# Transposing the latent mixer's probabilities in float32r, from a copy made by DMA

## The chip, the cores and the metric

One core of a Trainium2 chip runs one program. The metric is the device time in microseconds of one execution. The engines of the core are TensorE (PE in the profile, its weight loads PEld), VectorE (DVE), ScalarE (ACT), GpSimd (POOL) and SyncE (SP); DMAs are issued from the queues of SP, ScalarE and GpSimd. TensorE writes to PSUM, and its operands come from the SBUF.

## The reference, cut to what matters

The program runs two blocks on 512 tokens of width 1024 with 256 context tokens. The first block has two layers (attention, a gated linear recurrence, an MLP). The second has two mixers, of which the first is the latent mixer. Queries, keys and values of 16 heads come out of low-rank projections, tokens attend to context and tokens, the context attends to itself, and the result is gated and projected:

```python
def mla_mixer(hc, hx, row, col, w_in, q_norm_g, w_uq, kv_norm_g, w_ukv, w_out):
    ...
    oc = attention_blocks(qc, kc, vc)
    ox = attention_blocks(qx, jnp.concatenate([kc, kx], axis=1), jnp.concatenate([vc, vx], axis=1))

    def out(o, gate):
        b, n = gate.shape[:2]
        return (o.reshape(b, n, MLA_WIDTH) * jax.nn.silu(gate)) @ w_out
```

`attention_blocks` is a softmax of the scores (96 features a head, 32 of them rotated) times the values (64 a head). All arithmetic of the reference is float32. In the kernel the probabilities have to be transposed, because the product with the values contracts over the keys, which then must lie on the partitions.

## The kernel before

Most products are made from operands that are split into two float32r parts, high and low. `split` (L248) copies the high part on ScalarE (L251, L254) and subtracts it on VectorE (L252, L255); `mm3` (L278) makes three TensorE products of each pair, lines L280 to L282. The profile prints float32r operands of TensorE as f32.

`mla` (L1050 and on) has a first stage (low-rank projections and gates) and then the attention, which the change touches. It runs over eight pairs of heads `hp` and, for each, five steps: one for the context (`c` = 1: two tiles of 128 queries against 256 keys, for each head), then four for the tokens (one tile of 128 queries against 768 keys). So there are 40 steps of two heads, and 80 tiles of probabilities `p`. In a step

- `softmax` (L1199) makes the scores of one head into a PSUM tile `S` (L280 to L282), the row maximum on VectorE (`mx`, L1211), the exponential on ScalarE into `p` with its row sum (L1216), the reciprocal of the sum (L1218) and the scaling of `p` in place (L1221), both on VectorE;
- `weigh` (L1225) works on the step before: for each head it transposes `p` in blocks of 128x128 on TensorE into a PSUM tile `T` (L1236; `p` is the weight, the identity streams), copies the result on ScalarE into `pt` (L1237), and then makes the products with the values into `O` (L1244). At the end of a pair's queries the gate `sg` is multiplied in (L1251);
- `prepare` (L1136), in pieces between these, makes keys and queries of the next pair: it loads and splits weights (`raw`, L264, from SP's queue), makes the products into `T` tiles, and moves the rotated part `rot` into `qT` by four small copies within the SBUF, also from SP's queue (L1178).

Buffers: `p` has three, `pt` three, `S` two, `T` three and `O` one. The order of the code gives each instruction its priority. The framework's planner, which knows its own estimates of durations and landings, orders the instructions of each engine and of each DMA queue from that: an instruction whose operands it does not expect to be ready lets others go ahead. On the chip each engine then runs its instructions in this order and waits on semaphores. A TensorE instruction that waits holds those behind it.

The first block has an attention of its own with other functions (L488 and on), whose transposes (L516) the change leaves as they are. There the scores of a float32r product are padded to 256 columns (L489).

Of the kernel before, what the change touches and what calls it, by code (L numbers as in the profile page):

```python
# [11 lines left out]
F32R = mybir.dt.float32r  # L12
I32 = mybir.dt.int32
U32 = mybir.dt.uint32
AF = mybir.ActivationFunctionType
# [177 lines left out]
def f32(ap):  # L193
    return ap.bitcast(F32)
# [855 lines left out]
def mla(P, xs, mod, H, before, keep):  # L1050

    nc, A = P.nc, P.A
# [13 lines left out]
    with ExitStack() as s1:  # L1066
# [33 lines left out]
        for j in range(8):  # L1100
            w = W().rearrange("p s (k n) -> p s k n", k=8)
            for c, o, n in PARTS:
                ps = P.bankA()[:, 0:n]
# [7 lines left out]
    with st as s2:  # L1111
        P.psum(s2, S=(2, 2), T=(3, 1), O=(1, 1))
        kp, pp, one, qp = (P.pool(*x, s2) for x in (("m2k", 3), ("m2p", 3), ("m2o", 1), ("m2q", 4)))
        kTs = [one.tile([96, 2, 768], F32R, name=f"kT{i}") for i in (2, 3, 0, 1)]
        kTs = kTs[2:] + kTs[:2]
        tab = one.tile([128, 512], F32, name="tab")
        nc.sync.dma_start(tab, A["k_gridT"])
        V = [vp.tile([128, 1024], F32, name="V") for _ in range(6)]

# [79 lines left out]
        def softmax(hp, c, t0):  # L1199
            two, m, c0 = (2, 256, 512) if c else (1, 768, 0)  # L1200
            ps = []
            for i in range(2):
                qT, kT = qTs[hp][i], kTs[(2 * hp + i) % 4]
                pss = P.bankS()
                for t in range(two):
                    q = slice(c0 + (t0 + t) * 128, c0 + (t0 + t + 1) * 128)
                    for o, w in ((512, 256),) if c else ((0, 512), (512, 256)):
                        d = pss[:, t * m + o - c0:t * m + o - c0 + w]
                        P.mm3(d, qT[:, 0, q], qT[:, 1, q], kT[:, 0, o:o + w], kT[:, 1, o:o + w], True, True)
                mx = P.sm.tile([128, 2], F32, name="mx")  # L1210
                nc.vector.tensor_reduce(mx[:, 0:two], pss[:, 0:two * m].rearrange("p (t n) -> p t n", t=two),  # L1211
                                        AX.X, OP.max, negate=True)
                p = pp.tile([128, 768], F32, name="p")
                sl = P.sm.tile([128, 2], F32, name="sl")
                for t in range(two):
                    nc.scalar.activation(p[:, t * m:(t + 1) * m], pss[:, t * m:(t + 1) * m], AF.Exp,  # L1216
                                         bias=mx[:, t:t + 1], accum_out=sl[:, t:t + 1])
                nc.vector.reciprocal(sl[:, 0:two], sl[:, 0:two])  # L1218
                for t in range(two):
                    v = p[:, t * m:(t + 1) * m]  # L1220
                    nc.vector.tensor_scalar(v, v, sl[:, t:t + 1], None, op0=OP.mult)  # L1221
                ps.append(p)
                yield ps

        def weigh(hp, c, t0, ps):  # L1225
            two, m, c0 = (2, 256, 512) if c else (1, 768, 0)
            if t0 == 0:
                weigh.o = P.bankO()
            pts = []
            for p in ps:  # L1230
                pt = kp.tile([128, 768], F32, name="pt")
                for o in range(0, two * m, 512):
                    w = min(512, two * m - o)
                    pst = P.bankT()
                    for k in range(0, w, 128):
                        nc.tensor.transpose(pst[:, k:k + 128], p[:, o + k:o + k + 128], P.ident)  # L1236
                    nc.scalar.activation(pt[:, o:o + w], pst[:, 0:w], AF.Copy)  # L1237
                pts.append(pt)
                yield
            for t in range(two):  # L1240
                for k in range(m // 128):
                    for i in range(2):
                        h = 2 * hp + i
                        nc.tensor.matmul(weigh.o[64 * i:64 * i + 64, (t0 + t) * 128:(t0 + t + 1) * 128],  # L1244
                                         V[4 * c + k][:, h * 64:(h + 1) * 64],
                                         pts[i][:, t * m + k * 128:t * m + (k + 1) * 128],
                                         start=(k == 0), stop=(k == m // 128 - 1))
            n = 256 if c else 512
            if (t0 + two) * 128 == n:
                v = sg[hp][:, c0:c0 + n]  # L1250
                nc.vector.tensor_tensor(v, v, weigh.o[:, 0:n], op=OP.mult)  # L1251
# [3 lines left out]
        for hp, c, t in steps:  # L1255
            if c:
                ready = prepare(hp + 1) if hp < 7 else iter(())
            sm = softmax(hp, c, t)
            w = weigh(*before) if before else iter(())
            next(w, None)  # L1260
            for _ in range(2):
                ps = next(sm)
                next(ready, None)
                next(w, None)
            before = (hp, c, t, ps)
        alternate(weigh(*before))


# [325 lines left out]
def program(tc, A, out):  # L1594
    with ExitStack() as ctx:
        P = Prog(tc, A, ctx)
        xs = [P.res.tile([128, 1024], F32, name=f"x{t}") for t in range(4)]
        before, keep = ExitStack(), ExitStack()
        H, mod = first_block(P, xs, P.pool("hx", 1, before))
        finish = mla(P, xs, mod.m[0], H, before, keep)  # L1600
        gla(P, xs, finish, keep, mod.m[1], out)
# [18 lines left out]
```

## Time and profile before

| | |
|---|---|
| median of 3 runs | 2333.55 us (2333.11 to 2333.55) |
| the profiled execution | 2335.07 us, its span 2333.3 us |
| TensorE busy | 2284.1 us, 98% |
| VectorE, ScalarE busy | 1478.0 us (63%), 1063.0 us (46%) |
| DMA | 234.38 MB, mean 100 GB/s |
| attention of the latent mixer | about 1685 to 1935 us of the span |

A busy time adds up the instructions of an engine, overlaps counted once. TensorE's instructions overlap: a product starts while the one before it still runs, so their distance from start to start tells what one costs. A group line gives the count, the busy time, the mean duration of one, and the idle time of the engine just before with what ended it. In a timeline, instructions of one kind that follow each other are merged, with their count and the length from the first start to the last end.

### The profile page before, as it was taken

The page shows a single profiled execution, that of the slowest core. Times are in us where ns is not written, and L with a number is a line of the kernel's source. Part 1 is how long each engine was busy: PE and PEld are TensorE (multiplying, and loading weights), DVE is VectorE, ACT ScalarE, POOL GpSimd, SP SyncE. Part 2 cuts the span into 40 slices and gives each one's busy share as a digit, 9 for nine tenths or more (in the row PEclk, how much of TensorE's full clock was granted, in tenths as well). Part 3 has the DMA queues.
Part 4 walks back from the last instruction along what each step waited for, and adds up shares of the span by engine and source line. Part 5 has one row for each costly group of instructions (what it writes and reads, how often), then busy time and mean ns, then how long its engine had stood idle before and what let it go on. Part 6 is the DMA issues. An engine that isn't in the chain of part 4 may idle for free.

```text
span 2333.3 us, 30784 instructions
## 1 busy us (share of the span) xinstructions
PE 2284.1 (98%) x12108; PEld 1875.9 (80%) x12108; DVE 1478.0 (63%) x2556; ACT 1063.0 (46%) x1958; POOL 71.4 (3%) x120
## 2 busy tenths in 40 slices
PE   8999999999999999999999999999999999999998
PEld 6777878888888777788888888888888888788886
DVE  4477796555555547779645556564478776756586
ACT  3366423444443235642344445452477772563332
POOL 0000000000000000000000000010000000000000
PEclk9999999999999999999999999999999999999999
DMA  4221464555642322146454554212110121121112
GB/s 162 81 73 55 145 212 142 167 130 151 174 100 91 92 81 75 52 155 216 135 172 120 160 164 116 92 54 72 49 31 21 24 74 37 54 81 37 55 46 72
DMA packets 61312, 234.38 MB, mean 100 GB/s; under 512 B 8544, under 2 KB 9840, under 8 KB 54768
## 3 DMA queue, kind: packets, MB, share of 16 engines
q1 hardware_dynamic: 50512, 179.99, 23.3%
q0 software_dynamic: 3456, 25.17, 6.0%
q10 hardware_dynamic: 7200, 27.27, 3.7%
q8 instruction: 95, 1.56, 0.3%
q14 instruction: 49, 0.40, 0.1%
HBM read 227.15 MB, written 2.10 MB: 98 GB/s over the span
## 4 chain that ended last, share of the span: by engine, by line
PE 81%; DVE 10%; ACT 3%; DMA 3%; issue 2%; POOL 1%; SPq 0%; POOLq 0%; ACTq 0%; DVEq 0%
PE A L282 18%; PE A L281 18%; PE A L280 18%; PE S L280 4%; PE S L282 4%; PE S L281 4%; PE O L1244 2%; DVE spl L252 2%; PE T L1236 2%; PE O L522 1%; DMA ada<-in_ada 1%; PE S L496 1%; DVE junk L933 1%; PE T L516 1%; ACT spl L251 1%
## 5 line engine op out<-in xcount | busy, mean ns | idle before, releaser
L280 PE MATMUL A<-big,spl 128*128 128x512 f32 (+1 forms) x1280 | 482.2, 377 | 1.9 <-DVE x L768 1.2
L282 PE MATMUL A<-big,spl 128*128 128x512 f32 (+1 forms) x1280 | 481.0, 376 | 0.2 <-DVE spl L252 0.2
L281 PE MATMUL A<-big,spl 128*128 128x512 f32 (+1 forms) x1280 | 480.1, 375 | 0.0
L252 DVE TENSOR_TENSOR spl<-raw,spl 128x1024 fp32r<-128x1024 f32 (+2 forms) x265 | 317.2, 1200 | 184.0 <-ACT spl L251 182.2
L251 ACT ACTIVATE spl<-raw 128x1024 fp32r<-128x1024 f32 (+2 forms) x265 | 275.2, 1040 | 292.2 <-PE A L282 190.6
L282 PEld LDWEIGHTS A<-big,spl 128*128 128x128 f32 x1280 | 241.2, 188 | 44.6 <-issue 2.6
L280 PEld LDWEIGHTS A<-big,spl 128*128 128x128 f32 x1280 | 241.3, 189 | 43.9 <-DVE x L768 1.6
L281 PEld LDWEIGHTS A<-big,spl 128*128 128x128 f32 x1280 | 241.3, 189 | 42.5 <-issue 1.4
L252 DVE TENSOR_TENSOR spl<-quarter,spl 128x1024 fp32r<-128x1024 f32 x84 | 102.2, 1223 | 144.9 <-ACT spl L251 144.9
L280 PE MATMUL A<-spl,big 128*128 128x512 f32 (+2 forms) x480 | 182.7, 384 | 3.7 <-DVE tg L668 2.1
L281 PE MATMUL A<-spl,big 128*128 128x512 f32 (+2 forms) x480 | 182.3, 381 | 1.4 <-DVE spl L252 0.8
L282 PE MATMUL A<-spl,big 128*128 128x512 f32 (+2 forms) x480 | 181.7, 380 | 0.2 <-DVE ms L289 0.2
L251 ACT ACTIVATE spl<-quarter 128x1024 fp32r<-128x1024 f32 x84 | 88.2, 1057 | 97.4 <-PE S L282 41.1
L280 PEld LDWEIGHTS A<-spl,big 128*128 128x128 f32 x480 | 90.2, 189 | 23.2 <-DVE tg L668 3.0
L281 PEld LDWEIGHTS A<-spl,big 128*128 128x128 f32 x480 | 90.7, 189 | 18.9 <-DVE spl L252 3.4
L282 PEld LDWEIGHTS A<-spl,big 128*128 128x128 f32 x480 | 90.6, 189 | 16.7 <-issue 1.1
L280 PE MATMUL S<-spl,part 128*128 128x512 f32 x264 | 102.8, 389 | 0.0
L281 PE MATMUL S<-spl,part 128*128 128x512 f32 x264 | 102.8, 389 | 0.0
L282 PE MATMUL S<-spl,part 128*128 128x512 f32 x264 | 102.8, 389 | 0.0
L1211 DVE TENSOR_REDUCE mx<-S 128x1 f32<-128x768 f32 (+1 forms) x80 | 71.8, 900 | 26.5 <-PE S L282 25.7
L291 POOL TENSOR_TENSOR rstd<-ms,mhalf 128x1 f32<-128x1 f32 (+2 forms) x68 | 44.2, 650 | 1247.5 <-DVE ms L289 1203.2
L1237 ACT ACTIVATE pt<-T 128x512 f32<-128x512 f32 (+1 forms) x144 | 66.4, 501 | 32.4 <-PE T L1236 31.2
(442 smaller groups left out, 4349.2 us busy)
## 6 DMA issues: line engine op xcount, KB each, us to landing
raw<-in_wl SPq DMA_DIRECT2D x196, 512.0 KB, 3.7
ada<-in_ada ACTq DMA_DIRECT2D x48, 512.0 KB, 4.0
quarter<-in_wq SPq DMA_DIRECT2D x24, 1024.0 KB, 6.2
quarter<-in_wq POOLq DMA_DIRECT2D x24, 1024.0 KB, 8.7
raw<-in_gla SPq DMA_DIRECT2D x33, 512.0 KB, 3.4
raw<-in_mla SPq DMA_DIRECT2D x20, 512.0 KB, 3.5
raw<-in_mla SPq DMA_DIRECT2D x8, 384.0 KB, 3.0
qT<-rot SPq DMA_DIRECT2D x32, 96.0 KB, 2.8
```

The lines of the kernel that those rows point to most:

```text
L251: nc.scalar.activation(hi, src, AF.Copy)
L252: nc.vector.tensor_tensor(lo, src, f32(hi), op=OP.subtract)
L280: mm(ps, lh, rh, start=start, stop=False, **more)
L281: mm(ps, lh, rl, start=False, stop=False, **more)
L282: mm(ps, ll, rh, start=False, stop=stop, **more)
L291: nc.gpsimd.tensor_tensor(r, ms, self.mhalf[:, 0:w], op=OP.pow)
L496: nc.tensor.matmul(banks[hh][:, 0:w], qT[hs, i, q], kT[hs, j, 0:w], start=(i + j == 0), stop=(i == 1))
L516: nc.tensor.transpose(psp[:, k * 128:(k + 1) * 128], p[:, k * 128:(k + 1) * 128], P.ident)
L1211: nc.vector.tensor_reduce(mx[:, 0:two], pss[:, 0:two * m].rearrange("p (t n) -> p t n", t=two), AX.X, OP.max, negate=True)
L1236: nc.tensor.transpose(pst[:, k:k + 128], p[:, o + k:o + k + 128], P.ident)
L1237: nc.scalar.activation(pt[:, o:o + w], pst[:, 0:w], AF.Copy)
L1244: nc.tensor.matmul(weigh.o[64 * i:64 * i + 64, (t0 + t) * 128:(t0 + t + 1) * 128], V[4 * c + k][:, h * 64:(h + 1) * 64], pts[i][:, t * m + ...
```

## The change

Each scaled tile `p` is copied by a DMA from SP's queue, within the SBUF, into a tile `p2` of type float32r; the DMA sees both as float32, so the bits stay as they are. The transposes read `p2` and an identity in float32r, and write to the same PSUM tile, seen as float32r. `p2` has three buffers of its own. The identity in float32r is made once on ScalarE. Nothing else changes; the copy out of PSUM and the product with the values stay in float32.

```diff
         kp, pp, one, qp = (P.pool(*x, s2) for x in (("m2k", 3), ("m2p", 3), ("m2o", 1), ("m2q", 4)))
+        pp2 = P.pool("m2r", 3, s2)
...
+        ident_r = one.tile([128, 128], F32R, name="ident_r")
+        nc.scalar.activation(ident_r, P.ident, AF.Copy)
...
                 for t in range(two):
                     v = p[:, t * m:(t + 1) * m]
                     nc.vector.tensor_scalar(v, v, sl[:, t:t + 1], None, op0=OP.mult)
-                ps.append(p)
+                p2 = pp2.tile([128, 768], F32R, name="p2")
+                nc.sync.dma_start(f32(p2)[:, 0:two * m], p[:, 0:two * m])
+                ps.append(p2)
                 yield ps
...
                     for k in range(0, w, 128):
-                        nc.tensor.transpose(pst[:, k:k + 128], p[:, o + k:o + k + 128], P.ident)
+                        nc.tensor.transpose(pst[:, k:k + 128].bitcast(F32R), p[:, o + k:o + k + 128], ident_r)
                     nc.scalar.activation(pt[:, o:o + w], pst[:, 0:w], AF.Copy)
```

## Rows read from the trace of the kernel before

**Rows 1.** The page, parts 1 and 2: busy time, clock in 40 slices

```profile
PE 2284.1 (98%) x12108; PEld 1875.9 (80%) x12108; DVE 1478.0 (63%) x2556; ACT 1063.0 (46%) x1958; POOL 71.4 (3%) x120
...
PEclk9999999999999999999999999999999999999999
```

**Rows 2.** Busy time by stretch; columns in the first line

```profile
core 0: us, PE busy (x) PEld busy (x) DVE busy (x) ACT busy (x) POOL busy (x), PEclk, DMA share, GB/s
1685.00:1935.00 250.00, 247.42 (x2080) 208.19 (x2078) 192.39 (x367) 181.19 (x412) 0.00 (x0) 1.00 0.14 36
```

**Rows 3.** Line L1236, the transposes: count, duration min/median/max ns

```profile
L1236 PEld LDWEIGHTS T<-ident,p x448: 137/140/145, 1685.8 to 1931.4; 128*128 128x128 f32 x150
L1236 PE MATMUL T<-ident,p x448: 269/273/330, 1685.8 to 1931.5; 128*128 128x128 f32 x150
```

**Rows 4.** TensorE in order of time: start, length, line, operands, count

```profile
1764.30 0.40 PE L281 MATMUL S<-kT,qT 96*128 96x512 f32 x1
1764.54 0.82 PE L1236 MATMUL T<-ident,p 128*128 128x128 f32 x6
1765.11 0.47 PE L282 MATMUL S<-kT,qT 96*128 96x512 f32 x1
```

**Rows 5.** Float32r (printed f32): two products of that timeline; load, mean ns

```profile
1775.55 0.28 PE L280 MATMUL T<-ckT,spl 128*128 128x256 f32 x1
1775.67 0.28 PE L281 MATMUL T<-ckT,spl 128*128 128x256 f32 x1
...
L280 PEld LDWEIGHTS S<-kT,qT 96*128 96x128 f32 x156 | 29.5, 189 | 8.1 <-issue 4.1 <-ACT p L1216 1.8 <-ACT pt L1237 0.2
```

**Rows 6.** Plain float32, 128 columns: one group of L1488, seven records in order

```profile
L1488 PE MATMUL L<-qk,ka x104: 270/276/377, 2114.3 to 2262.8; 128*128 128x128 f32 x104
...
2129.23 0.94 PE L1488 MATMUL L<-qk,ka 128*128 128x128 f32 x7
```

**Rows 7.** DMA issues: count, KB, median us to landing; those into qT

```profile
raw<-in_wl SPq DMA_DIRECT2D x196, 512.0 KB, 3.7
...
raw<-in_mla SPq DMA_DIRECT2D x20, 512.0 KB, 3.5
raw<-in_mla SPq DMA_DIRECT2D x8, 384.0 KB, 3.0
qT<-rot SPq DMA_DIRECT2D x32, 96.0 KB, 2.8
...
DMA to landing us min/median/max: 2.7/2.8/4.0
```

**Rows 8.** One step, all engines in order of time

```profile
1765.98 0.96 DVE L1211 TENSOR_REDUCE mx<-S 128x1 f32<-128x768 f32 x1 [0.54 <-PE S L282]
...
1767.23 0.90 ACT L1216 ACTIVATE p<-S,mx 128x768 f32<-128x768 f32 x1
...
1767.56 1.53 PE L1244 MATMUL O<-pt,V 128*64 128x128 f32 x24
...
1768.73 0.62 DVE L1221 TENSOR_SCALAR p<-p,sl 128x768 f32<-128x768 f32 x1
...
1769.59 0.82 PE L1236 MATMUL T<-ident,p 128*128 128x128 f32 x6
```

**Rows 9.** Waits of ScalarE for weight loads: us in total, times, longest

```profile
ACT spl L251 <- DMA raw<-in_wl: 42.0, 21, 4.3
...
ACT spl L251 <- DMA raw<-in_mla: 1.7, 2, 0.9
```

**Rows 10.** SP's queue in order of time

```profile
1739.72 3.00 SPq L1178 DMA_DIRECT2D qT<-rot  x4
1742.81 51.99 SPq L264 DMA_DIRECT2D raw<-in_mla  x3
```

**Rows 11.** The end of the attention on TensorE

```profile
1929.82 0.84 PE L1236 MATMUL T<-ident,p 128*128 128x128 f32 x6 [0.41 <-DVE p L1221]
1930.42 0.48 PE L280 MATMUL A<-spl,hi 128*128 128x512 f32 x1
```

## The prediction

> **What bounds the kernel now.** The page comes first. TensorE is busy 98% of the span, VectorE 63%, ScalarE 46%, and the granted clock is at its upper level, 2.4 GHz, in all forty slices [rows 1]. So the kernel is bound by TensorE almost everywhere, and a change counts only by what TensorE then does less, or by where it now waits. Next the table by stretches, for the one that the change touches: the attention of the latent mixer, 1685 to 1935 us. There TensorE is busy 247.4 of 250.0 us at a clock of 1.00, VectorE 192.4, ScalarE 181.2 and the DMA engines 14% of the time [rows 2]. So TensorE has 2.6 us of slack in 250, and the other engines have far more.
>
> Then line L1236, the transposes. There are 448 (16 heads, each 4 plus 24 blocks of 128x128), of 273 ns each, with a weight load of 140 ns [rows 3]. Matmuls overlap, so a duration is not a price. The price is the distance from start to start: six in a row take 0.82 us, so (0.82 - 0.273) / 5 = 0.109 us [rows 4]. All of them cost 448 x 0.109 = 49 us of TensorE.
>
> Last the order in time. In the code the three products of a score stand together; in the trace six transposes stand between the second (L281) and the third (L282) [rows 4]. The framework's planner thus puts each transpose where it expects `p`, and lets other ready work go ahead of it. This decides what the copy costs.
>
> **The change: transposes.** The count stays 448; only the spacing can change. No row shows a transpose in float32r, nor any float32r product of under 256 columns, so I bound it. From below: a float32r product streams 256 columns with starts 0.12 us apart and 0.28 us long [rows 5], what a float32 transpose needs for 128. Half of it is 0.06 us, a saving of 0.049. From above: a float32r weight load of 128 columns takes 189 ns [rows 5] where the transpose's takes 140 [rows 3]; if `p` as a float32r weight needs the longer load, the load sets the pace at about what it is now, and nothing is saved. One row pulls to each end and neither is nearer, so I take the middle: 0.0245 us, x 448 = 11.0 us less, with ends 0 and 22.0. A worse case stands among the rivals.
>
> A rule of the Trainium skill bears on this. The rows: a plain float32 product of 128 columns is two records (L1488 has 224 of them, of which one group stands, for 112 products in the code), and seven records take 0.94 us, so (0.94 - 0.276) / 6 = 0.111 each and 0.222 for a product [rows 6]; the transpose's 0.109 is half of that. The Trainium skill (TensorE: Matmul & The Clock Gate, Terms) says that transpose mode is four times faster for float32. By the measured rows it is twice. If the missing factor of two is what float32r brings, a transpose takes 0.055 us; that is what rival (a) works out from rows.
>
> **The change: copies.** It adds 80 DMAs on SP's queue, 16 of 256 KB and 64 of 384 KB, each between the scaling of `p` (L1221) and its transposes. A copy within the SBUF of 96 KB lands 2.8 us after its issue (2.7 to 4.0), a load of 384 KB in 3.0 and one of 512 KB in 3.5 [rows 7]. I take 3.0 us, with ends 2.7 and 4.0. Is that on the path? In a step without other work (5.05 us from one group of transposes to that of the next step, 1764.54 and 1769.59 [rows 4, 8]) the chain from the end of a score through maximum, exponential, reciprocal and scaling to the transpose takes 1769.59 - 1765.98 = 3.6 us [rows 8]; with the copy it is 6.6. To cover it the transposes must move behind later work: one whole step (5.05) plus the second head's score (about 1.1) plus a group of O products (about 1.4) lie ahead of them then, some 7.5 us of TensorE work, 0.9 more than needed. The buffers allow it. `p` is held from its exponential (1767.23) to the landing (1769.35 + 3.0), 5.1 us, at two per step 2.0 of its 3 buffers; `p2` from the issue to the end of its transposes, about 4.9 us, 1.9 of 3. So in steady state the copy is hidden by the next step's scores and products, and if this cover were gone, up to 3.0 us per step would show.
>
> What shows is the part by which a landing is later than the planner booked. The rows for that: ScalarE waited 42.0 us for the 196 weight loads of the first block and 1.7 us for the 28 larger ones of this mixer [rows 7, 9]. That is 0.21 us a load there and 0.06 here. I take this mixer's, since its DMA engines are as empty as the copies will find them: 80 x 0.06 = 5 us. The ends are 0 and 80 x 0.21 = 17.
>
> SP's queue: the copies wait there for VectorE, and behind them stand weight loads and the copies of `rot` into `qT`. Three loads are spread over 52 us and each is read much later, so a hold of 3 us is covered; `qT` is needed only by the next pair of heads. The other way round, four `qT` issues hold SP 3.0 us [rows 10]; a copy caught behind them lands that much later. There are 8 such groups; this belongs to the 17 us end.
>
> The rest. At the end of the stage there is no next step to hide behind: the last transposes follow `p` at 1929.82, and products of the next stage are already drawn in between them (1930.42) [rows 11]. Up to 3.0 us could show there; with more of those products to draw in I take 1.0. `ident_r` is one small ScalarE copy outside the chain, hidden by products on TensorE and under half a microsecond without them. ScalarE's copies out of PSUM keep their shape.
>
> Sum: -11.0 + 5.0 + 1.0 = -5.0 us. The profiled execution took 2335.07 us (span 2333.3 and 1.8 around it), 1.5 above the median of 2333.55. So 2330.1 on its own scale, and 2328.5 against the median, from which the cases below are counted too.
>
> **The rivals.** (a) Transposes at half the spacing: -22.0 + 6.0 = -16.0, 2317.5. For it: float32r streams at half of float32's time. Against it: the longer weight load.
>
> (b) No faster transposes, the change does not do what it says: 0 + 6.0, 2339.5. For it: the weight load's row. Against it: these loads overlap with products, and a transpose's own load is the shorter kind.
>
> (c) The copy shows, the case on the slow side. The place is TensorE's wait at L1236 for the landing of `p2`. It decides from the point where a landing is later than the booking: the planner gives a transpose no more room than it expects (0.2 us now between scaling and transpose [rows 8]), and TensorE runs in order behind it. Each microsecond is paid in each of 40 steps, 40 us. With one microsecond the time is 40 + 1 - 11 = +30, 2363.5; with half of one, 2343.5. For it: `qT` copies that took up to 4.0 us, and SP's 3 us groups. Against it: 1.7 us of waits for this mixer's loads.
>
> (d) A float32r product of only 128 columns costs what a plain float32 one does, 0.222 us: 448 x 0.113 = +50.6, +56.6 with the waits, 2390. For it: nothing in the trace excludes it, since the first block streams 256 columns in float32r even where 128 would do (L489) and products of 128 columns are in float32. Against it: a transpose in float32 costs half of the plain product, so the plain product's price need not hold for transposes.
>
> **How the numbers follow.** Chances: forecast 0.38 (2323 to 2334, with the transposes' saving between a quarter and three quarters of its range, 5.5 to 16.5 us), (a) 0.18, (b) 0.16, (c) 0.20, (d) 0.08. A measurement of this kernel can tell 0.2%, 4.7 us, from no change, so faster means below 2328.9. Faster: 0.21 of the forecast and all of (a), 0.39. Same (2328.9 to 2338.2): 0.17 of the forecast, 0.07 of (b) and 0.02 of (c), 0.26. Slower: the rest of (b) and (c), and (d), 0.35. The two signs are close, because a gain of 11 us stands against waits of which only the small end is visible in this mixer. The range of 8 in 10 goes from 2315, below (a), to 2362, the middle of (c); it leaves out (d), the worse half of (c) and little of (a).
>
> **What would show it.** In the changed kernel the spacing of L1236 within a group of six: about 0.085 us by the forecast, 0.06 by (a), 0.109 by (b), over 0.2 by (d). The idle time of TensorE before L1236 that a DMA into `p2` ends: some 5 us in all by the forecast, 20 to 40 by (c). The landing of `p2`: about 3.0 us. The order: each pair of transposes behind both scores of the next step. The attention should end about 5 us earlier, with everything ahead of 1660 us and behind it unchanged; a difference elsewhere would make the account wrong, and so would a granted clock below 1.00 in this stretch.

## The result, and the profile after

| | before | after |
|---|---|---|
| median, timed together | 2333.38 us (2333.11 to 2333.55) | 2359.78 us (2357.62 to 2363.43) |
| ratio | | 1.0115, 95% interval 1.0097 to 1.0132 |
| span of the profiled execution | 2333.3 us | 2356.0 us |
| products with the values, first to last start | 1690.0 to 1933.8 us | 1693.0 to 1958.0 us |

The changed kernel is slower by 26.4 us. The last line of the table is from the views of the tile `O`, before and after: the products with the values start 3 us later and end 24 us later. The lines moved: the transposes are L1241 (were L1236), the maximum L1214, the exponential L1219, the scaling L1224, the copy out of PSUM L1242, the values L1249; the new DMA is L1226, and the profile calls its two tiles `p<-p`.

Busy time by stretch in the changed kernel; columns as in [rows 2]. The first line has that group's stretch, the second ends where the attention now ends.

```profile
1685.00:1935.00 250.00, 233.57 (x1888) 190.60 (x1888) 178.65 (x342) 166.48 (x381) 0.00 (x0) 0.99 0.41 143
1685.00:1958.00 273.00, 253.47 (x2072) 206.46 (x2070) 190.06 (x365) 179.45 (x410) 0.00 (x0) 0.99 0.41 141
```

TensorE, which had 2.6 us of slack in 250, is without work for 16.4 us in the same stretch, and for 19.5 in the longer one. The DMA engines are busy 41% of the time instead of 14%, and the clock is no longer at 1.00 throughout.

The transposes themselves, by their source line: durations min/median/max in ns (before: [rows 3]), and the idle time of TensorE just before them by what ended it.

```profile
L1241 PEld LDWEIGHTS T<-ident_r,p x448: 137/141/228, 1688.9 to 1955.9; 128*128 128x128 f32 x150
L1241 PE MATMUL T<-ident_r,p x448: 223/250/329, 1689.2 to 1955.9; 128*128 128x128 f32 x150
...
  DMA p<-p: 10.2, 13
```

The load is as short as that of a float32 transpose (141 against 140 ns), and the product has become shorter (250 against 273). The 10.2 us that a copy ended in 13 waits are the sum of the weight loads' waits and the products', which are largely the same stretches of time seen twice; the products alone give 5.0 us in 7 waits (below).

The issues of the copies: KB each, median us from issue to landing.

```profile
p<-p SPq DMA_DIRECT2D x64, 384.0 KB, 2.6
...
p<-p SPq DMA_DIRECT2D x16, 256.0 KB, 2.3
```

So the copies are quick, and TensorE seldom waits for one. What it waits for is in the list of waits from 1660 to 1965 us: engine, tile and line, releaser, then us in total, times, longest.

```profile
DVE mx L1214 <- PE S L282: 35.4, 27, 4.7
ACT p L1219 <- DVE mx L1214: 34.4, 41, 2.0
...
PEld S L280 <- ACT p L1219: 14.8, 20, 2.5
PE S L280 <- ACT p L1219: 11.1, 18, 2.3
...
PEld T L1241 <- DMA p<-p: 5.2, 6, 2.2
...
PE T L1241 <- DMA p<-p: 5.0, 7, 2.0
```

Of the kernel before, the same list from 1660 to 1965 us has

```profile
PEld S L280 <- ACT p L1216: 1.8, 3, 0.9
PE S L280 <- ACT p L1216: 1.1, 3, 0.7
```

A line of PEld is the wait of a weight load and one of PE that of a product, and the load and the product of one place wait through the same stretch. So the two must not be added: the place below shows one stretch that counts as 2.52 us for the load and as 2.32 for the product. Of TensorE's idle time the products' lines tell, and those are used from here on. The expectations further down add both (26 us for 14.8 + 11.1), so their figures for waits are some two times the idle time.

The largest waits of TensorE are not at the transposes, 5.0 us, but at the first product of a score, L280, for the exponential: 11.1 us, and 1.1 before. These 10 us more and the 5.0 are 15 of the 17 us by which TensorE's idle time has grown. The other 7 of the 24 us by which the values end later are not idle time: at most 3.4 us are the stretches at the lower clock shown below (an estimate: half of the 6.9 us that the two last), and the rest was not measured apart. A score needs a free `S` tile; there are two, and one comes free when the exponential has read it. VectorE and ScalarE wait more too: the maximum 35.4 us for scores (25.7 before) and the exponential 34.4 us for the maximum (12.8 before). Both have time to spare on average; when scores come in lots, the reading is, they first stand still and then are late for two at once.

The first and longest such place, all engines in order of time:

```profile
1685.26 0.39 PE L280 MATMUL S<-kT,qT 96*128 96x512 f32 x1
...
1685.91 1.14 DVE L252 TENSOR_TENSOR kT<-T,kT 64x256 fp32r<-64x256 f32 x2
...
1686.18 0.28 PE L282 MATMUL S<-kT,qT 96*128 96x256 f32 x1
...
1686.98 1.53 DVE L1214 TENSOR_REDUCE mx<-S 128x2 f32<-128x512 f32 x2
...
1688.17 0.46 ACT L1219 ACTIVATE p<-S,mx 128x256 f32<-128x256 f32 x1
...
1688.77 0.19 PEld L280 LDWEIGHTS S<-kT,qT 96*128 96x128 f32 x1 [2.52 <-ACT p L1219]
1688.77 0.60 PE L280 MATMUL S<-kT,qT 96*128 96x512 f32 x1 [2.32 <-ACT p L1219]
1689.16 0.67 PE L1241 MATMUL T<-ident_r,p 128*128 128x128 f32 x4
```

TensorE has made the next step's first score right behind the last one, instead of transposes, and would make another. The `S` tile for it still holds a score whose maximum VectorE has started at 1686.98, behind the splitting of keys, and whose exponential begins at 1687.70 and 1688.17. TensorE stands still for 2.32 us.

The granted clock around this place, by stretches of 4 us (TensorE's busy time and count, clock, DMA share, GB/s):

```profile
1684.00:1688.00 4.00, 2.46 (x15) 1.00 0.23 75
1688.00:1692.00 4.00, 3.23 (x15) 0.63 0.45 115
1692.00:1696.00 4.00, 3.53 (x17) 0.94 0.42 114
1696.00:1700.00 4.00, 4.00 (x33) 1.00 0.42 169
```

After that gap the clock is for some 3 us at its lower level of 1.2 GHz, and the same products take longer: the transposes at 1689.16 need 0.67 us for four, against 0.46 to 0.54 at 2.4 GHz elsewhere. There is one more such dip, from 1908 to 1916 us, behind an idle time of 1.16 us at the same kind of place. Not every such idle time is followed by one: in copy_only and in order_all_no_copy (below) TensorE stands still at this very place for 2.32 and 2.33 us, and the clock stays at 1.00 in the 4 us behind it. The Trainium skill (TensorE: Matmul & The Clock Gate, A second HAM failure mode: psum-queue depth-cycling) tells of a kernel in which short idle times between groups of products, from cycling through PSUM, lowered the clock again and again. This trace agrees in part: an idle time at a PSUM tile stands ahead of both dips, but they are only two, about 3.4 us each, while the scores waited 18 times.

In TensorE's order, a score stood directly behind another score 3 times in the 80 of the kernel before; in the changed kernel it does 30 times. That is a sign of an uneven order and not its price, since it is 40 times in copy_only and 17 in two_behind, which loses nothing (both below). Theory A is that this order costs the time, through the two `S` tiles. The rivals B to H, each named where it is tested, are the copies' traffic and queue (B), the float32r transposes (C), the late landing itself (D), an order that is a mistake of the planner (E), the buffers of `p2` (F), a gain of the shift by a step that covers up an unchanged loss (G) and the switches and the clock of an irregular order (H).

### The profile page after: what moved, and what is told of

It is laid out like the page before. It is cut to its first block, busy times and chain, and to the rows that moved or that the text cites. A ratio compares the mean times of both kernels' runs of the same rounds, so it can differ in the third digit from the quotient of the medians.

```text
span 2356.0 us, 31073 instructions
## 1 busy us (share of the span) xinstructions
PE 2290.2 (97%) x12108; PEld 1873.4 (80%) x12108; DVE 1475.9 (63%) x2556; ACT 1062.0 (45%) x1959; POOL 71.4 (3%) x120
## 3 DMA queue, kind: packets, MB, share of 16 engines
q1 hardware_dynamic: 62032, 209.36, 26.1%
## 4 chain that ended last, share of the span: by engine, by line
PE 79%; DVE 10%; ACT 4%; DMA 3%; issue 3%; POOL 1%; SPq 0%; ACTq 0%; POOLq 0%; DVEq 0%
PE A L282 17%; PE A L281 17%; PE A L280 17%; PE S L280 4%; PE S L281 3%; PE S L282 3%; PE O L1249 2%; DVE spl L252 2%; PE O L522 1%; DMA ada<-in_ada 1%; PE T L1241 1%; PE S L496 1%; DVE junk L933 1%; PE T L516 1%; PE T L280 1%
## 5 line engine op out<-in xcount | busy, mean ns | idle before, releaser
L280 PE MATMUL A<-big,spl 128*128 128x512 f32 (+1 forms) x1280 | 481.8, 376 | 2.0 <-DVE x L768 1.2
L280 PEld LDWEIGHTS A<-big,spl 128*128 128x128 f32 x1280 | 241.1, 188 | 44.6 <-DVE x L768 1.6
L280 PE MATMUL A<-spl,big 128*128 128x512 f32 (+2 forms) x480 | 182.5, 384 | 4.1 <-DVE tg L668 2.4
L280 PEld LDWEIGHTS A<-spl,big 128*128 128x128 f32 x480 | 90.1, 189 | 23.6 <-DVE tg L668 3.3
L280 PE MATMUL S<-spl,part 128*128 128x512 f32 x264 | 102.7, 389 | 0.0
L1214 DVE TENSOR_REDUCE mx<-S 128x1 f32<-128x768 f32 (+1 forms) x80 | 71.6, 900 | 36.8 <-PE S L282 35.4
L1219 ACT ACTIVATE p<-S,mx 128x768 f32<-128x768 f32 (+1 forms) x96 | 72.6, 759 | 39.5 <-DVE mx L1214 34.4
```

What stands on the lines that cost most here:

```text
L280: mm(ps, lh, rh, start=start, stop=False, **more)
```

## The experiments

Each median stands beside that of the kernel before, timed together with it; ratios have their 95% interval.

### One part alone

**transposes_only**: no copy, the scaling writes the float32r tile.

```diff
-                    nc.vector.tensor_scalar(v, v, sl[:, t:t + 1], None, op0=OP.mult)
-                p2 = pp2.tile([128, 768], F32R, name="p2")
-                nc.sync.dma_start(f32(p2)[:, 0:two * m], p[:, 0:two * m])
+                    nc.vector.tensor_scalar(p2[:, t * m:(t + 1) * m], v, sl[:, t:t + 1], None, op0=OP.mult)
```

> No copy: VectorE's scaling writes p2, a float32r tile with buffers of its own, and the transposes read that in float32r. (The scaling thus rounds the probabilities to float32r; no instruction or copy is added otherwise.) Theory A, the order: the float32r transposes are as cheap as their spacing of 0.085 us says, and all of the loss is the copy's, so here 448 x 0.024 = 10.5 us go and the time is about 2323, at a clock of 1.00 throughout the attention. Rival B, the copies' traffic and their queue: the same 2323. Rival C, the float32r transposes themselves break up TensorE's stream (switches from transposes to scores cost 5 us and from scores to transposes 4 us more than before, and the clock dips): 2333 to 2345, with the dips of the clock.

Measured: 2328.92 against 2333.00 us, 0.9983 (0.9974 to 0.9992), with the clock at 1.00 in the stretch. The clock does not dip, and a score's products wait 1.5 us for the exponential (1.1 before), so rival C falls; but only 4.1 us are gained, not 10.5. Three lines of TensorE's order in time tell why (start, length):

```profile
1768.12 0.64 PE L1240 MATMUL T<-ident_r,p 128*128 128x128 f32 x6
1768.59 0.46 PE L282 MATMUL S<-kT,qT 96*128 96x512 f32 x1
1768.89 0.28 PE L280 MATMUL S<-kT,qT 96*128 96x256 f32 x1
```

In the kernel before the second product behind the same group, which follows the three lines of [rows 4], is

```profile
1765.42 0.28 PE L280 MATMUL S<-kT,qT 96*128 96x256 f32 x1
```

Six transposes stand (0.64 - 0.25) / 5 = 0.08 us apart here; the median of all 358 gaps within groups is 0.085, as in the changed kernel, and 0.109 before. But the score behind them starts 0.08 us after the last transpose (1768.59 - 1768.51), where it started 0.02 to 0.03 us after the last float32 one (1765.11 - 1765.09 in [rows 4]; the medians over all groups are 0.086 and 0.028). From the first transpose to the second product behind the group it is 0.77 us here, and 0.88 in the kernel before (1764.54 to 1765.42). So 0.11 us are saved in a group of six, 0.018 a transpose and not 0.0245, in all 8.2 us, an estimate from this one place. The other 4 us were not found in one place.

**copy_only** and **copy_unread**: the copy goes to a float32 tile; the transposes read that copy, or `p` itself, in float32.

```diff
-                p2 = pp2.tile([128, 768], F32R, name="p2")
-                nc.sync.dma_start(f32(p2)[:, 0:two * m], p[:, 0:two * m])
-                ps.append(p2)
+                p2 = pp2.tile([128, 768], F32, name="p2")
+                nc.sync.dma_start(p2[:, 0:two * m], p[:, 0:two * m])
+                ps.append(p2)            # copy_unread: ps.append(p)
```

> The copy alone: it goes into a float32 tile, and the transposes read that copy in float32 with the float32 identity. Theory A: all of the loss stays and the 10.5 us of the cheaper transposes are missing, 2360 + 10.5 = about 2370, with the waits of the scores for the exponential (26 us in the changed kernel) still there. Rival B: the same. Rival C: much less than the changed kernel, 2335 to 2345.

> The copies are made as in the changed kernel, 80 of them from SP's queue into three float32 tiles, but nothing reads them: the transposes read p in float32, as before. Theory A: what costs is that the transposes have to come later, not the transfer, so within 4 us of 2333. Rival B, traffic of 28 MB, SP's queue and the longer life of p: most of the loss, 2350 to 2370. Rival C: 2333.

Measured: copy_only 2363.17 against 2333.00, 1.0134 (1.0119 to 1.0149); copy_unread 2333.57, 1.0006 (0.9996 to 1.0015). So the copy that is read costs 30 us and the same copy unread nothing that can be measured. Rival B (traffic, SP's queue, the longer hold of `p`) falls. The two parts add up: +30.2 and -4.1 make +26.1, and +26.4 was measured. (copy_only stays 7 us under its 2370 because the float32r transposes are worth 4.1 us in time and not 10.5.)

### More room for the copy

**two_behind** makes transposes and values two steps behind the scores; **five_p2** only has its buffers; **two_behind_plain** has the shift without copy and in float32.

```diff
-            w = weigh(*before) if before else iter(())
+            w = weigh(*before.pop(0)) if len(before) > 1 else iter(())
...
-            before = (hp, c, t, ps)
+            before.append((hp, c, t, ps))
```

> The changed kernel, but the code makes transposes and products with the values of the step before last, not of the last one, and p2 has five buffers for that. A copy then has a whole step more of room, about 5 us. Theory A: scores need not run ahead of schedule any more, TensorE's order becomes regular again (one score, one group of transposes), the waits for the exponential fall from 26 us to under 8, and most of the loss goes: 2323 to 2335, 2328 the middle. Rival B: nothing changes, 2355 to 2365. Rival C: the switches stay, 2350 to 2360.

> The changed kernel with five buffers for p2 instead of three and nothing else; two_behind (2331.3 us) has them too. Theory A: S, not p2, is what TensorE runs out of, so 2353 to 2365 as the changed kernel. Rival F, the buffers: they were two_behind's gain, so 2331 to 2340.

> The kernel before, float32 transposes of p and no copy, but as in two_behind the code makes transposes and products with the values of the step before last, and p has six buffers. Theory A: the shift by itself is worth nothing, 2330 to 2336, and two_behind hides all but 2 of the copy's 30 us. Rival G: the shift is a gain of its own that covers up a copy that still costs its 30 us: then about 2331 - 30 + 4 = 2305 here.

Measured: two_behind 2331.25 against 2333.00, 0.9993 (0.9983 to 1.0002); five_p2 2356.01 against 2333.89, 1.0093 (1.0078 to 1.0109); two_behind_plain 2330.31 against 2333.89, 0.9986 (0.9976 to 0.9995). Buffers alone bring hardly anything, so rival F falls. With a step more of room the loss is gone, and with it the waits. In two_behind a score's products wait 1.1 us for the exponential instead of 11.1, as little as before, and the transposes 0.2 us for a DMA (1.2 at their loads):

```profile
PEld S L280 <- ACT p L1219: 3.8, 15, 1.0
...
PEld T L1241 <- DMA p<-p: 1.2, 4, 0.4
PE S L280 <- ACT p L1219: 1.1, 2, 0.8
```

Theory A had said that all but 2 us of the copy would be hidden. That was too much: the shift is a small gain of its own (two_behind_plain), and against the same shift without a copy (rounded_two_behind, below) the copy still costs some 10 us, by the two ratios 0.9993 - 0.9951.

The trace of two_behind shows something that the theory had not said. Between the score of a tile and its transposes TensorE completes one other score in 71 of the 80 tiles of the kernel before, one to four in the changed kernel, and three in 71 tiles of two_behind. So scores run further ahead there than in the changed kernel, with the same two `S` tiles, and hardly wait. The starts of the scores are 3.0 us apart with a standard deviation of 1.5 (before 3.1 and 1.5, changed kernel 3.3 and 2.1). What costs is thus not that scores run ahead but that they do so unevenly.

### The order alone, and the copy without the order

**order_no_copy** is transposes_only with TensorE's 1640 instructions of the attention held in the changed kernel's order; **order_all_no_copy** holds ScalarE's and VectorE's too. **copy_in_time** is the changed kernel in the order of transposes_only. `ORDER` lists places in the order of the code; the added edges set the order of issue and add no wait.

```diff
+        traced = nc.cur_bb.bb.instructions
+        first = len(traced)
         steps = [(hp, c, t) for hp in range(8) for c, t in ((1, 0), (0, 0), (0, 1), (0, 2), (0, 3))]
...
         alternate(weigh(*before))
+        mine = [i for i in traced[first:] if i.engine == mybir.EngineType.PE and "Mat" in type(i).__name__]
+        ranked = [mine[k] for a, n in ORDER for k in range(a, a + n)]
+        for x, y in zip(ranked, ranked[1:]):
+            P.tc.add_manual_dep(y, x.name, mybir.DependencyInfo(mybir.DependencyClass.NoSync, ...), reason="order")
```

> The kernel without the copy (transposes_only, 2328.9 us; its scaling rounds the probabilities to float32r), but with TensorE's 1640 instructions of the attention held by hand in the order that they have in the changed kernel. No DMA stands between scaling and transpose. Theory A, the order: TensorE loses its time because scores stand ahead of transposes two at a time, and then wait for one of the two S tiles until the exponential has read it. The order alone then brings most of the copy's 30 us: 2345 to 2360, with 15 to 25 us of waits of a score's first product for the exponential. Rival D, the copies' landing: the time goes because p2 comes late, directly or through what follows from it; without the copy it is 2326 to 2335 in any order.

> A sharper form of order_no_copy, in which ScalarE and VectorE kept an order made for a kernel without copies (scores waited 34 us for the exponential there against 26 in the changed kernel, and the clock was at 0.94 against 0.99 in the stretch). Here the attention's instructions on TensorE, ScalarE and VectorE are all held by hand in the order of the changed kernel, and there is no DMA between scaling and transpose (the scaling rounds the probabilities to float32r). What differs from the changed kernel is the landing of the copies alone. Theory A: the order has most of the 31 us between transposes_only (2328.9) and the changed kernel (2359.8); what the transposes wait for DMAs there, 10 us, and what follows from it goes: 2343 to 2353, with 15 to 26 us of waits of a score for the exponential. Rival D, the landings: 2326 to 2335, waits for the exponential under 8 us. If the copies' landing costs nothing even indirectly: 2356 to 2362.

> The reverse: the changed kernel with its copies, but TensorE's instructions of the attention in the order that they have without the copy (transposes_only), each group of transposes where p would be ready and p2 is not. In a quiet step the second head's score ends 3.6 us before its transposes; with 2.7 us for the landing and about 1 us to the end of the next score of that head a step takes about 7.4 us where it took 5.05. Steps with preparation have some 2 us of room. Theory A: running ahead is the cheaper way, and this one is slower than the changed kernel: 40 steps of 1 to 2.4 us over 2329, so 2370 to 2425, with most of the loss as waits of the transposes for the DMA. Rival E, the new order is the mistake, and waiting would have been cheap: 2335 to 2350.

Measured: order_no_copy 2356.14 against 2333.89, 1.0098 (1.0077 to 1.0119); order_all_no_copy 2358.73 against 2333.48, 1.0108 (1.0091 to 1.0125); copy_in_time 2425.34 against 2333.89, 1.0396 (1.0370 to 1.0422). Without any DMA between scaling and transposes, the order of the changed kernel costs as much as the changed kernel. Its waits, in order_all_no_copy:

```profile
ACT p L1296 <- DVE mx L1291: 36.4, 38, 2.2
DVE mx L1291 <- PE S L282: 34.5, 26, 4.7
...
PEld S L280 <- ACT p L1296: 17.3, 23, 2.5
PE S L280 <- ACT p L1296: 12.7, 20, 2.3
```

These are the changed kernel's waits, at a score's products 1.6 us larger (12.7 against 11.1), and those for a DMA are gone. The third case of its expectation holds, and theory A's 2343 to 2353 does not: the landings that do come late cost nothing beside this that can be told from the uncertainty of some 4 us of each ratio (rival D falls). Some 2 us of the equality may be the clock, 0.98 between 1685 and 1958 us against 0.99. In order_no_copy, where the other two engines kept another order, a score's products waited 15.1 us and the clock was at 0.94 between 1685 and 1935 us, so its nearly equal time is in part a coincidence; order_all_no_copy is the one to go by.

In copy_in_time TensorE's wait for the copies is there as such. The waits of the transposes (L1261 there), from 1660 to 2060 us:

```profile
PE T L1261 <- DMA p<-p: 48.2, 36, 3.0
...
PEld T L1261 <- DMA p<-p: 32.5, 19, 2.7
```

That is 48 us of idle time. With it the clock is at 0.89 between 1685 and 1935 us, which at half speed in the low stretches is worth up to 27 us there, an estimate. The time is just above the end of the expected range (2425). So the planner's detour, 26 us, is the cheaper of two bad choices; waiting in the old order costs 91. Rival E falls.

### The hold of an S tile

**after_no_max** and **before_no_max** leave the maximum out, with TensorE's order held as in the changed kernel and as in the kernel before. Their probabilities are others, of a 64th of the scores; they serve for the time alone.

```diff
-                mx = P.sm.tile([128, 2], F32, name="mx")
-                nc.vector.tensor_reduce(mx[:, 0:two], ..., AX.X, OP.max, negate=True)
...
-                                         bias=mx[:, t:t + 1], accum_out=sl[:, t:t + 1])
+                                         scale=1 / 64, bias=P.zero, accum_out=sl[:, t:t + 1])
```

> The changed kernel with its copies and with TensorE's order in the attention held by hand as it is there, but the row maximum is left out: the exponential is taken of a 64th of the score, without a bias, and so can start as soon as the score is done. An S tile is held about 1.2 us less. Theory A, the two S tiles: the waits of a score for the exponential fall from 26 us to under 6, and the time from 2359.8 to 2331 to 2343; what remains over before_no_max are the dearer switches of the irregular order and a few waits for copies. Rival D, the landing of the copies: 2350 to 2360. Rival H, the irregular order costs by its switches and the clock alone, whoever waits: 2348 to 2358.

> The control: the kernel before, TensorE's order held as it is there, with the row maximum left out in the same way (exponential of a 64th of the score, no bias). There a score waits only 1.8 + 1.1 us for the exponential in all, so all theories say 2329 to 2334; if it falls by more, the maximum matters to the time by another way than the S tiles, and after_no_max has to be read against this one.

Measured: 2341.94 against 2334.90, 1.0029 (1.0018 to 1.0040), and 2330.99 against 2334.90, 0.9985 (0.9975 to 0.9995). The distance between the two kernels falls from 26.4 to 11.0 us when an `S` tile is held a microsecond less, in the same order of TensorE; rivals D and H expected times of 2348 and more, 17 above this control. The waits of a score's products for the exponential fall from 11.1 to 3.0 us:

```profile
PEld O L1277 <- ACT pt L1270: 8.5, 19, 0.7
...
PEld S L280 <- ACT p L1247: 4.3, 7, 1.3
...
PE O L1277 <- ACT pt L1270: 3.0, 9, 0.6
PE S L280 <- ACT p L1247: 3.0, 3, 1.1
```

By the count of the expectation, loads and products added, that is 7.3 us, a little over its 6. The clock is at 1.00 in the stretch. Leaving the maximum out does two things, though: an `S` tile is held for less time, and VectorE has 80 tiles' reductions less to do and so is less behind. The runs do not separate the two, and none has a third `S` tile; that it is the number of `S` tiles is read from the waits.

What is left has a part of the same kind: the products with the values wait 3.0 us for ScalarE's copies out of `T` (8.5 at their loads; 0.4 and 2.6 in before_no_max). How the remaining 11 us divide between that, the dearer changes from one kind of product to another and the waits that stayed is open.

### A faster version

**rounded_two_behind** is transposes_only and two_behind together, so without a copy.

> Transposes_only and two_behind together, the candidate that could beat both kernels: no copy, the scaling writes p2 in float32r (which rounds the probabilities), transposes in float32r, transposes and products of the step before last, five buffers of p2. If the two gains add up (2328.9 against 2333.0, and two_behind_plain's 2330.3 against 2333.9): 2324 to 2328.

Measured: 2323.51 against 2334.90 us, 0.9951 (0.9937 to 0.9966), the fastest of all, 0.5% below the kernel before, and a little more than the two gains together (0.9983 x 0.9986 = 0.9969). Against two_behind_plain the float32r transposes are worth 0.9986 - 0.9951 = 0.35%, 8 us, which is what 448 x 0.018 gives; each of the two ratios is uncertain by some 3 us.

## Why the prediction was wrong

**The forecast** was 2328.5 us, -5.0; the result is +26.4. The range (2315 to 2362) held the time, by way of a rival whose mechanism was not the one at work; that was luck.

**Bounds now.** Right: TensorE sets the time, and the 24 us by which the values end later are nearly all in the span of the profiled execution (22.7 us longer). One reading was loose: the digits of [rows 1] show only 0.90 or more of each slice; for the stretch it is [rows 2] that shows 1.00.

**Transposes, -11.0.** Right in kind, too large in size. The spacing came out at 0.085 us, the middle that was taken. But the price of a group is not its spacing times its count. It ends when the next product can start, and after float32r transposes that is 0.06 us later. The term was 8.2 us by that account, 4.1 by the time of transposes_only, and about 8 in the steadier order of rounded_two_behind. The end of 22 and rival (a) are out, as are (b), since something was saved, and (d). The end of nothing rested on a load of 189 ns; the load measured 141. The four times of the Trainium skill (TensorE: Matmul & The Clock Gate, Terms) are not reached in float32r either: against the plain float32 product's 0.222 us the spacing of 0.085 is 2.6 times faster.

**Copies, landing.** 3.0 us were taken, 2.6 and 2.3 measured; the median lies below the lower end of 2.7, and the longest landing (4.4) above the upper end of 4.0. The Trainium skill (SBUF — State Buffer, The DMA setup-cost knee) gives about 2 us and the bytes over 436 GB/s, an estimate of 2.9 and 2.6 us; both copies land 0.3 us sooner than that.

**Copies, "hidden by the next step's scores and products".** This is the step that failed. It put the move of the transposes at nothing, having counted TensorE's work behind which a transpose can move (7.5 us, 6.6 needed) and the buffers of `p` and `p2`. Three of `p2` were enough, as five_p2 shows; with three of `p` the exponential waited 3.0 us for copies, and no run has more of them beside the copy. The step took for granted that every group of transposes moves by the same distance. The planner's order is not like that: of the 78 tiles that have a next step, 49 have their transposes behind both of its scores, and the others have them earlier. Scores then come in lots. An `S` tile is held from the first product of the score, about 1.1 us of TensorE's time, through the maximum (0.96) and the exponential (0.90), 3 us and more with the waits between, so a score that comes too soon behind two others finds neither tile free. In the even order of before a score's products waited 1.1 us for that, in the new one 11.1, and order_all_no_copy loses 25 us by this order without any copy. The cover that was counted does exist: in two_behind, where all 78 tiles have their transposes behind both scores of the next step, the loss is gone with the same two `S` tiles.

**Waits, +5.0.** TensorE's idle time that copies ended was 5.0 us at the transposes (5.2 at their loads, largely the same time), so this term came out as it was sized. By order_all_no_copy it added nothing to the total that can be told, since the time was lost in the order anyway.

**SP's queue, `ident_r`.** As predicted: copy_unread has all of that and costs nothing.

**The tail, +1.0**, was not measured apart.

**Rival (c)** gave 2343.5 to 2363.5, and the result lies there. Its mechanism did not decide, though: it asked for 20 to 40 us of waits for DMAs before the transposes, and there were 5. What it describes is copy_in_time, with 48 us of such waits and 2425 us. The planner avoids it, and pays in another place.

**What would show it.** Three of the signs came out as named or nearly so (spacing, landing, 5 us of waits for copies), and they are no evidence for the sum. The order did not: 49 of 78 tiles. This sign and the last ones told: a clock below 1.00 in the stretch, and an attention that ended later.

## What to carry to other kernels

When a new latency is to be hidden by running other work ahead, ask not only whether there is enough of it, but also whether it will come evenly. Work that runs ahead by the same distance in every step needs no more `S` tiles here (two_behind); work that comes in lots waits for them, from their first write to their last reader (the changed kernel). Where the schedule is a planner's, the cheapest way to hide a latency may be to say so in the code: one more step between producer and consumer made the distance even and brought the loss of 26 us down to the time of before. And waits of weight loads and of products are not to be added: a sum above TensorE's whole idle time shows the mistake. Last, the price of a group of products is the time to the next product behind it, not its count times its spacing.

## What was not expected of the hardware

After float32r transposes the next product starts 0.086 us (median) after the start of the last one, after float32 transposes 0.028 us, though the spacing within the group is the smaller one. 80 copies of 256 and 384 KB within the SBUF, at 41 to 45% of the DMA engines' time, moved the time of copy_unread by 0.6 us, not more than can be told from nothing. And an idle time of TensorE of 2.3 us was followed by about 3 us at 1.2 GHz in the changed kernel, but not at the same place in copy_only and order_all_no_copy, so such a gap can cost more than itself and need not.
